# First layer's FFN: up projections of 18 of 22 tiles by a seven-product block scheme, on one NeuronCore

## The chip, the cores and the metric

The kernel runs on one core of one Trainium2 chip. The metric is the device time of one execution in microseconds (us). Before the change it is 2640.16 us, the median of three runs (2639.87 to 2642.24). Five engines work beside each other: TensorE (PE in the profile, its weight loads PEld) multiplies matrices, VectorE (DVE) and ScalarE (ACT) work on elements and can read TensorE's results in PSUM, GpSimd (POOL) works on elements in SBUF and issues some DMAs, and SyncE (SP) issues most DMAs. Each engine runs its own list of instructions in order and waits for others by semaphores.

## The reference

Two layers of a hybrid transformer block, width 1024. Each layer has a token mixer and, after it, the gated feed-forward network (FFN) that the change is about. Layer 1 of the text (index 0 in the code) applies the FFN to 512 latent tokens and 256 context tokens with the same weights, so the kernel handles them as 768 columns; layer 2 applies it to the 512 latent tokens alone.

```python
D_MODEL, SEQ, CTX_LEN, DEPTH = 1024, 512, 256, 2
FFN_HIDDEN = 2816                       # 22 tiles of 128

def swiglu(h, w1, w3, w2):
    return (jax.nn.silu(h @ w1) * (h @ w3)) @ w2

for l in range(DEPTH):
    ...                                 # shift, scale and gate from c @ w_ada[l]; mixer sub-layer
    if not last:
        ctx = ctx + cg_f * swiglu(modulate(rms_norm(ctx, norm_ffn[l]), csh_f, csc_f), w_ffn1[l], w_ffn3[l], w_ffn2[l])
    x = x + g_f * swiglu(modulate(rms_norm(x, norm_ffn[l]), sh_f, sc_f), w_ffn1[l], w_ffn3[l], w_ffn2[l])
return rms_norm(x, final_norm)
```

## The kernel before

**Layout.** Activations stand transposed: 128 channels on the partitions, tokens in the columns. The normalized input h of the FFN is one tile [128, 2, 8, 768]: eight chunks of 128 channels, each twice, as a high part rounded to fp32r and as the remainder, the low part. Weights are split the same way after loading: `wload` (L225) fetches 128x512 pieces (four chunks of one 128-column tile, 256 KB) through SP's queue, and `wsplit` (L218) makes the high part on ScalarE (L220) and the low part on VectorE (L222). There are three buffers for raw pieces and four each for high and low parts. `mm3` (L521 to L527) multiplies by three products per chunk: high by high, high by low, low by high. All accumulate in one PSUM bank.

**The FFN.** `ffn_up` (L1576) makes one of 22 hidden tiles: w1 and w3 columns are loaded and split, then for each of two column halves (0 to 384, 384 to 768) 24 matmuls for the gate, a Silu on ScalarE (L1583), 24 matmuls for the value, the product on VectorE (L1586), and the split of the result into a g tile (L1587, L1588). Five PSUM banks ("f") go round. The hidden tiles form three groups of 8, 7 and 7; after each group a down projection runs over eight column tiles n: it loads w2 for the group's chunks, multiplies them with the g tiles and adds the result, scaled, onto the residual xT (`resid`, L1547). In the first group the first NSF = 3 tiles are done for the latent tokens 0 to 512 first and then for 512 to 768, so that the normalization of the second range hides beside the first. In the last group the down projection runs over all n for columns 0 to 512 and then over all n for 512 to 768; between the two `norm_range` is called on columns 0 to 512 for layer 2's input (a new h tile), so that it runs beside the second range's matmuls. `norm_range` squares and sums on ScalarE and VectorE, sums over partitions on TensorE (L196), takes the power on GpSimd (L169), broadcasts by transposes (L201), and then makes h chunk by chunk (multiply on VectorE, L207; scale and shift, L177, and cast, L180, on ScalarE; low part on VectorE, L181).

**Beside the FFN** runs the modulation of layer 2, `ada_steps` (L111), a generator: each step takes one 128x512 piece of w_ada out of one of two buffers, multiplies it into one or two accumulators on VectorE (L130), and issues the next load on SP's queue (L119). After eight pieces the accumulators are transposed on TensorE (L144) and reduced on VectorE (L145). Three blocks follow each other: the first has two live rows, the others one. `ada_next(n)` takes n steps: NAF = 3 behind each up tile, NAN = 2 inside each down tile n, and what is left before the last down projection.

**Order of work.** Instructions are put into each engine's list by a scheduler that takes, of those that a simulated timeline calls ready, the one that comes first in the program; so work can run ahead of its place where its engine is free and its buffers are. Buffers are given out at the first use and are free after the last. The `ga` tag has six buffers [128, 2, 768] and `gm` eight; they hold the mixer's output for `w_out` and then the g tiles.

```python
groups = [list(range(0, 8)), list(range(8, 15)), list(range(15, 22))]
...
ws = wload(w_ffn2[l], grp_[0] * P, n * P, len(grp_))
ada_next(NAN)
for lo, hi in rngs:
    pu = gbank()[:, :hi - lo]
    mm3(pu, ws, lambda k: gt[k][:, 0, lo:hi], lambda k: gt[k][:, 1, lo:hi])
    resid(pu, n, lo, hi, 40)
```

Of the kernel before, what the change touches and what calls it, by code (L numbers as in the profile page):

```python
# [10 lines left out]
F32 = mybir.dt.float32  # L11
F32R = mybir.dt.float32r
AF = mybir.ActivationFunctionType
# [5 lines left out]
P = 128  # L19
D = 1024  # L20
NC_ = D // P
# [19 lines left out]
NTS = (2, 2)  # L41
AJ = 2
NAF = 3
NAN = 2
NSF = 3
NSL = 4
WB = (0, 3)
PRE = (0.9, 0.9, 0.6, 0.5, 0.5)
# [14 lines left out]
def block_kernel(ctx: ExitStack, tc: tile.TileContext, x, c, ctx_in, c_ctx, w_ada, b_ada, norm_mix, w_in,  # L63
# [12 lines left out]
    def ttile(n=512, name="t"):  # L76
        t = tp.tile([P, 512], F32, tag="t", name=name)
        return t[:, :n]
# [542 lines left out]
    for l in range(DEPTH):  # L621
# [881 lines left out]
        with ExitStack() as st:  # L1503
# [3 lines left out]
            def gbank():  # L1507
                return pf.tile([P, 512], F32, tag="f", name="pf", bufs=5)
# [1 line left out]
            def tbank():  # L1510
                return pf.tile([P, 512], F32, tag="T", name="pT", bufs=2)

            gp.tile([P, 512], F32, tag="tf", name="tf", bufs=2)
            gp.tile([P, 512], F32, tag="wada", name="wada", bufs=4)
            gp.tile([P, 2, NT], F32R, tag="ga", name="g", bufs=6)
            if last:
                deep = {"ws": 8, "wh": 3, "wl": 3}
                for tag, n in deep.items():
# [9 lines left out]
            gcount = [6]  # L1528

            def gtile(name):  # L1530
                i = gcount[0] % 14
# [3 lines left out]
            mg = [gtile("mg") for n in range(NC_)]  # L1535
            xT = []
            for lo, hi in oh:
                for n in range(NC_):
# [29 lines left out]
            def ada_next(n):  # L1568
                for _ in range(n):
                    if ada:  # L1570
                        try:
                            next(ada[0])
                        except StopIteration:
                            ada.pop(0)

            def ffn_up(f, g, rngs):  # L1576
                w1 = wload(w_ffn1[l], 0, f * P, NC_)
                w3 = wload(w_ffn3[l], 0, f * P, NC_)
                for lo, hi in rngs:
                    p1 = gbank()[:, :hi - lo]  # L1580
                    mm3(p1, w1, lambda k: h[:, 0, k, lo:hi], lambda k: h[:, 1, k, lo:hi])
                    t = gp.tile([P, 512], F32, tag="tf", name="tf", bufs=2)[:, :hi - lo]
# [5 lines left out]
                    nc.vector.tensor_sub(g[:, 1, lo:hi], t, g[:, 0, lo:hi])  # L1588

            def finish(lo, hi):  # L1590
                nt = (hi - lo) // P
# [28 lines left out]
                    yield  # L1620

            groups = [list(range(0, 8)), list(range(8, 15)), list(range(15, 22))]
            for gi, grp_ in enumerate(groups):
                gt = []
                for f in grp_:
# [2 lines left out]
                if gi == 0 and last:  # L1628
                    todo = [(grp_[:NSL], [r]) for r in oh] + todo[NSL:]
                elif gi == 0:  # L1630
                    todo = [(grp_[:NSF], [r]) for r in oh] + todo[NSF:]
                for fs, rngs in todo:
                    nr = iter(())
                    if gi == 0 and rngs == [oh[0]]:
                        nr = norm_range(tbank, xT, h, mod, 32, 24, *oh[1])
                        next(nr)
                    for f in fs:
                        ffn_up(f, gt[f - grp_[0]], rngs)
                        next(nr, None)
                    drain(nr)  # L1640
                    if f:
                        ada_next(NAF)
                lastg = gi == len(groups) - 1
                if lastg:
                    for a in ada:
# [80 lines left out]
```

## Time and profile before

| what | value |
|---|---|
| median of three runs | 2640.16 us |
| profiled execution | 2639.56 us |
| its span, first to last instruction | 2637.8 us |
| TensorE busy | 2559.7 us, 14651 matmuls |
| VectorE busy | 1712.7 us |
| ScalarE busy | 1129.8 us |
| GpSimd busy | 114.1 us |
| granted TensorE clock, mean | 0.992 |
| FFN of layer 1, about | 998 to 1553 us of the span |

The profile is of one execution. Busy time is the time in which an engine has an instruction in work; TensorE's matmuls overlap, so their mean durations are longer than the distance of their starts. The span is cut into 40 slices for the digits, 9 is 90% or more busy. The chain that ended last is followed back from the last instruction: at each step to what released it, or to the instruction before it on its engine.

In the FFN of layer 1 the stages are: the first group's tiles for two token ranges until about 1054 us, its other five tiles until 1137, its down projection until 1203, the second group's seven tiles until 1319, its down projection until 1377, the third group's tiles until 1493, the last down projection for columns 0 to 512 until 1533 and for 512 to 768 until 1553.

### The profile page before, as it was taken

The numbers are of one execution on the slowest core, as the hardware profiler recorded it, in microseconds if no ns is written. First come the engines' busy times: TensorE is split into PE (matmuls) and PEld (weight loads), VectorE is DVE, ScalarE is ACT, GpSimd is POOL, SyncE is SP. The second block draws the span as 40 slices with busy tenths as digits, with TensorE's granted clock in tenths as the row PEclk, the third lists the DMA queues.
The fourth block names the chain that finished last, engine by engine and source line by source line (L and its number), as shares of the span: only waits on it lengthen the run. The fifth ranks groups of instructions, "written<-read, shape, count | busy, mean of one in ns | idle before, by whom it ended". The sixth has DMA issues, their size and how long they took to land.

```text
span 2637.8 us, 38763 instructions
## 1 busy us (share of the span) xinstructions
PE 2559.7 (97%) x14651; PEld 2348.8 (89%) x14651; DVE 1712.7 (65%) x3042; ACT 1129.8 (43%) x2262; POOL 114.1 (4%) x179
## 2 busy tenths in 40 slices
PE   7999999999999999999999999999999999999998
PEld 5999889999999988999999988778888888988888
DVE  5967887787778667463453579987766635733335
ACT  5245556556522245212212254566655424722235
POOL 2000000010000000000000000100000000000000
PEclk9999999999999999999999999999999999999999
DMA  8211112222245355343343452111232235633333
GB/s 285 76 41 45 45 33 73 58 62 60 77 150 156 113 164 156 92 128 96 96 152 96 137 148 85 53 41 53 68 80 66 78 96 162 175 96 95 97 92 112
DMA packets 401760, 263.07 MB, mean 100 GB/s; under 512 B 15882, under 2 KB 369492, under 8 KB 401572
## 3 DMA queue, kind: packets, MB, share of 16 engines
q1 hardware_dynamic: 394292, 236.67, 30.3%
q0 software_dynamic: 7280, 23.93, 3.2%
q8 instruction: 115, 1.88, 0.3%
q14 instruction: 73, 0.60, 0.1%
HBM read 243.75 MB, written 8.91 MB: 96 GB/s over the span
## 4 chain that ended last, share of the span: by engine, by line
PE 86%; DVE 5%; ACT 3%; issue 3%; DMA 1%; POOL 0%; DVEq 0%; POOLq 0%; SPq 0%; ACTq 0%
PE pf L527 15%; PE pf L526 14%; PE pf L525 14%; PE pf L609 10%; PE pf L610 10%; PE pf L611 10%; PE pS L906 3%; PE pT L935 2%; PE pv L1345 2%; PE pv L1434 1%; ACT e L925 1%; DVE nm L912 1%; DMA wada<-in_w_ada_dram 1%; ACT rot L798 0%; DVE pt L938 0%
## 5 line engine op out<-in xcount | busy, mean ns | idle before, releaser
L220 ACT CAST wh<-ws 128x512 fp32r<-128x512 f32 (+1 forms) x432 | 260.5, 607 | 564.8 <-PE pf L526 483.3
L526 PE MATMUL pf<-h,wh 128*128 128x384 f32 (+2 forms) x1360 | 468.2, 346 | 0.7 <-DVE h L181 0.6
L525 PE MATMUL pf<-h,wh 128*128 128x384 f32 (+2 forms) x1360 | 466.1, 347 | 2.9 <-ACT tg L730 1.5
L527 PE MATMUL pf<-h,wl 128*128 128x384 f32 (+2 forms) x1360 | 467.0, 346 | 0.0
L609 PE MATMUL pf<-h,wh 128*128 128x384 f32 (+1 forms) x1280 | 459.6, 359 | 1.9 <-ACT tg L781 1.4
L611 PE MATMUL pf<-h,wl 128*128 128x384 f32 (+1 forms) x1280 | 449.1, 351 | 0.0
L610 PE MATMUL pf<-h,wh 128*128 128x384 f32 (+1 forms) x1280 | 448.1, 350 | 0.0
L222 DVE TENSOR_TENSOR wl<-ws,wh 128x512 fp32r<-128x512 f32 (+1 forms) x432 | 288.9, 674 | 243.2 <-ACT wh L220 237.9
L525 PEld LDWEIGHTS pf<-h,wh 128*128 128x128 f32 x1360 | 253.9, 188 | 23.6 <-ACT tg L730 1.7
L526 PEld LDWEIGHTS pf<-h,wh 128*128 128x128 f32 x1360 | 255.8, 188 | 20.7 <-DVE h L181 2.0
L527 PEld LDWEIGHTS pf<-h,wl 128*128 128x128 f32 x1360 | 255.3, 188 | 19.3 <-DVE wl L222 0.2
L565 ACT CAST wh<-ws 128x512 fp32r<-128x512 f32 x264 | 164.1, 623 | 235.1 <-PE pf L610 195.9
L609 PEld LDWEIGHTS pf<-h,wh 128*128 128x128 f32 x1280 | 241.8, 189 | 16.3 <-ACT tg L781 2.0
L610 PEld LDWEIGHTS pf<-h,wh 128*128 128x128 f32 x1280 | 242.0, 189 | 13.4 <-issue 0.7
L611 PEld LDWEIGHTS pf<-h,wl 128*128 128x128 f32 x1280 | 241.2, 188 | 13.4 <-issue 0.2
L572 DVE TENSOR_TENSOR wl<-ws,wh 128x512 fp32r<-128x512 f32 x264 | 181.3, 688 | 97.5 <-ACT wh L565 96.0
L703 DVE SCALAR_TENSOR_TENSOR ca<-ub,cols,ca 128x798 f32<-128x798 f32 (+1 forms) x240 | 215.4, 898 | 3.9
L130 DVE SCALAR_TENSOR_TENSOR wada<-wada,sil 128x512 f32<-128x512 f32 x224 | 162.7, 748 | 56.6 <-DMA wada<-in_w_ada_dram 55.3
L525 PE MATMUL pf<-g,wh 128*128 128x384 f32 (+2 forms) x584 | 198.7, 341 | 0.0
L527 PE MATMUL pf<-g,wl 128*128 128x384 f32 (+2 forms) x584 | 197.5, 339 | 0.7 <-DVE wl L222 0.7
L526 PE MATMUL pf<-g,wh 128*128 128x384 f32 (+2 forms) x584 | 197.3, 338 | 0.0
L937 ACT CAST pt<-pT 128x512 fp32r<-128x512 f32 (+1 forms) x216 | 92.0, 471 | 153.3 <-PE pT L935 152.7
(324 smaller groups left out, 4073.6 us busy)
## 6 DMA issues: line engine op xcount, KB each, us to landing
ws<-in_w_ffn_dram SPq DMA_DIRECT2D x284, 256.0 KB, 3.0
ws<-in_w_in_dram SPq DMA_DIRECT2D x248, 256.0 KB, 2.9
wada<-in_w_ada_dram SPq DMA_DIRECT2D x160, 256.0 KB, 2.9
ws<-in_w_out_dram SPq DMA_DIRECT2D x58, 256.0 KB, 3.5
ws<-in_w_ffn_dram SPq DMA_DIRECT2D x48, 192.0 KB
wada<-in_w_ada_dram SPq DMA_DIRECT2D x16, 512.0 KB, 6.9
khl<-khl POOLq DMA_DIRECT2D x40, 192.0 KB, 3.2
ws<-in_w_four_dram SPq DMA_DIRECT2D x16, 256.0 KB, 2.7
```

The lines of the kernel that those rows point to most:

```text
L130: nc.vector.scalar_tensor_tensor(accs[r], w, s, accs[r], op0=ALU.mult, op1=ALU.add)
L220: nc.scalar.copy(wh[:, :n], st[:, :n])
L222: lastv[0] = nc.vector.tensor_sub(wl[:, :n], st[:, :n], wh[:, :n]).ins
L525: nc.tensor.matmul(o, lhsT=wh, rhs=xh(k), start=(k == 0), stop=False)
L526: nc.tensor.matmul(o, lhsT=wh, rhs=xl(k), start=False, stop=False)
L527: nc.tensor.matmul(o, lhsT=wl, rhs=xh(k), start=False, stop=(k == n - 1))
L565: nc.scalar.copy(wh, u.raw[len(u.wh)])
L572: nc.vector.tensor_sub(wl, u.raw[i], u.wh[i])
L609: nc.tensor.matmul(o, lhsT=wh, rhs=xh(k), start=(k == 0), stop=False)
L610: nc.tensor.matmul(o, lhsT=wh, rhs=xl(k), start=False, stop=False)
L611: nc.tensor.matmul(o, lhsT=wl, rhs=xh(k), start=False, stop=(k == nk - 1))
L703: nc.vector.scalar_tensor_tensor(a, u, w, a, op0=ALU.mult, op1=ALU.add)
```

## The change

In layer 1 (`fast`) hidden tiles 4 to 21 are made in nine pairs by `ffn_pair`, each projection of a pair by `quad`. A quad sees the projection as a 2x2 block product: two output tiles, two halves of the input channels (four chunks each), two halves of 384 columns. Seven products of 4 chunks x 3 matmuls replace eight. On the weight side the sums of blocks (s1, s2, and the later a21 and s2) are made by four GpSimd operations on raw 128x512 pieces; on the activation side `prepare` makes T1 to T4 once from h (T1 in the place of one block of h) with GpSimd, VectorE and ScalarE. The products are put together from PSUM by additions on VectorE and a copy on ScalarE; banks A, B and C take a second or third product by accumulation after they have been read. Raw pieces and sums come from eight buffers (three `ws`, five `sq`). Silu and the product of gate and value work on quarters of 128x384 in a 768-column tile `ts`, and the split into g follows once for the whole tile.

Groups are now 6, 6, 6 and 4 tiles, g tiles have the six `ga` buffers only (the buffers of `gm` go to T2 to T4 and the pieces), and `prepare`'s scratch shares `ga`. The first NCV = 4 tiles are done as before in two token ranges. The modulation takes no step in a pair (NAQ = 0), five in each down tile (NAN = 5), three after each of the two plain passes. Layer 2 runs its FFN as before.

```diff
-NAN = 2
-NSF = 3
+NAN = 5
+NCV = 4
+NAQ = 0
...
+            def prepare():
...
+                def put(dst, v):
+                    nc.scalar.copy(dst[:, 0], v)
+                    nc.vector.tensor_sub(dst[:, 1], v, dst[:, 0])
...
+                t3, t2, t4 = [gp.tile([P, 2, 4, HT], F32R, tag="tb", name="tb", bufs=3) for _ in range(3)]
+                v, u = scratch(), scratch()
+                nc.gpsimd.tensor_sub(u, blk(1, 1, 1), blk(1, 0, 1))
+                nc.vector.tensor_sub(v, blk(0, 1, 1), blk(0, 0, 1))
+                nc.vector.tensor_add(v, v, u)
+                put(t3, v)
+                v2 = scratch()
+                nc.gpsimd.tensor_add(v2, v, blk(1, 0, 0))
+                nc.vector.tensor_add(v2, v2, blk(0, 0, 0))
+                put(t2, v2)
+                u4 = scratch()
+                nc.gpsimd.tensor_sub(u4, blk(1, 1, 0), v2)
+                nc.vector.tensor_add(u4, u4, blk(0, 1, 0))
+                put(t4, u4)
+                nc.gpsimd.tensor_sub(v2, blk(1, 1, 1), v2)
+                nc.vector.tensor_add(v2, v2, blk(0, 1, 1))
+                t1 = h[:, :, 0:4, HT:2 * HT]
+                put(t1, v2)
...
+            def quad(W, f, done):
...
+                a11 = raw(0, f * P)
+                a21 = raw(0, (f + 1) * P)
+                a22 = raw(4 * P, (f + 1) * P)
+                s1 = sqtile("s1")
+                nc.gpsimd.tensor_add(s1, a21, a22)
+                s2 = sqtile("s2")
+                nc.gpsimd.tensor_sub(s2, s1, a11)
+                a12 = raw(4 * P, f * P)
+                w = wsplit(a11, 4)
+                A = gbank()[:, :HT]
+                prod(A, w, tops["B11"], True, True)
+                p1 = ttile(HT, "p1")
+                nc.scalar.copy(p1, A)
+                w = wsplit(s2, 4)
+                nc.gpsimd.tensor_sub(a21, a11, a21)
+                B = gbank()[:, :HT]
+                prod(B, w, tops["T2"], True, True)
+                u2 = ttile(HT, "u2")
+                nc.vector.tensor_add(u2, B, p1)
+                w = wsplit(a12, 4)
+                prod(A, w, tops["B21"], False, True)
+                nc.gpsimd.tensor_sub(s2, a12, s2)
+                done(0, 0, A)
+                w = wsplit(a21, 4)
+                prod(B, w, tops["T3"], False, True)
+                u3 = ttile(HT, "u3")
+                nc.vector.tensor_add(u3, B, p1)
+                w = wsplit(s1, 4)
+                C = gbank()[:, :HT]
+                prod(C, w, tops["T1"], True, True)
+                nc.vector.tensor_add(u3, C, u3)
+                done(1, 1, u3)
+                w = wsplit(a22, 4)
+                prod(B, w, tops["T4"], False, True)
+                nc.vector.tensor_add(p1, B, p1)
+                done(1, 0, p1)
+                w = wsplit(s2, 4)
+                prod(C, w, tops["B22"], False, True)
+                nc.vector.tensor_add(u2, C, u2)
+                done(0, 1, u2)
...
+                quad(w_ffn1, f, gate)
+                ada_next(NAQ)
+                quad(w_ffn3, f, value)
+                ada_next(NAQ)
+                for t, g in zip(ts, (g0, g1)):
+                    nc.scalar.copy(g[:, 0], t)
+                    nc.vector.tensor_sub(g[:, 1], t, g[:, 0])
...
+            if fast:
+                groups = [list(range(0, 6)), list(range(6, 12)), list(range(12, 18)), list(range(18, 22))]
...
-                    todo = [(grp_[:NSF], [r]) for r in oh] + todo[NSF:]
+                    todo = [(grp_[:NCV], [r]) for r in oh]
+                elif fast:
+                    todo = []
...
+                if fast:
+                    if gi == 0:
+                        prepare()
+                    for f in grp_[NCV if gi == 0 else 0::2]:
+                        ffn_pair(f, gt[f - grp_[0]], gt[f + 1 - grp_[0]])
```

## Rows read from the trace of the kernel before

**Rows 1.** The page: TensorE's and others' busy time, TensorE's slices, the chain's shares
```profile
PE 2559.7 (97%) x14651; PEld 2348.8 (89%) x14651; DVE 1712.7 (65%) x3042; ACT 1129.8 (43%) x2262; POOL 114.1 (4%) x179
...
PE   7999999999999999999999999999999999999998
...
PE 86%; DVE 5%; ACT 3%; issue 3%; DMA 1%; POOL 0%; DVEq 0%; POOLq 0%; SPq 0%; ACTq 0%
```
**Rows 2.** Windows by stage: length, busy us (instructions) per engine, clock, DMA, GB/s
```profile
1036.00:1054.00 18.00, 17.74 (x120) 17.42 (x119) 12.05 (x21) 5.93 (x12) 0.00 (x0) 1.00 0.72 215
...
1137.00:1203.00 66.00, 66.00 (x384) 65.85 (x383) 43.39 (x80) 9.49 (x16) 0.00 (x0) 1.00 0.46 140
1203.00:1319.00 116.00, 116.00 (x673) 115.93 (x672) 41.52 (x70) 29.84 (x55) 0.00 (x0) 1.00 0.30 87
1319.00:1377.00 58.00, 58.00 (x336) 57.93 (x335) 35.04 (x65) 9.30 (x16) 0.00 (x0) 1.00 0.52 159
...
1533.00:1553.00 20.00, 19.25 (x157) 18.51 (x156) 13.97 (x27) 11.16 (x20) 2.35 (x3) 1.00 0.55 161
```
**Rows 3.** Timeline of TensorE, up tiles: start us, duration, instruction; 84 starts apart
```profile
1085.17 0.33 PE L525 MATMUL pf<-h,wh 128*128 128x384 f32 x1
...
1099.73 0.33 PE L525 MATMUL pf<-h,wh 128*128 128x384 f32 x1
```
**Rows 4.** Timeline of TensorE, last down projection: three and nine starts apart
```profile
1520.18 0.39 PE L525 MATMUL pf<-g,wh 128*128 128x512 f32 x1
...
1520.88 0.40 PE L525 MATMUL pf<-g,wh 128*128 128x512 f32 x1
...
1539.74 0.28 PE L525 MATMUL pf<-g,wh 128*128 128x256 f32 x1
...
1540.81 0.28 PE L525 MATMUL pf<-g,wh 128*128 128x256 f32 x1
```
**Rows 5.** Groups of VectorE instructions, 1000 to 1640 us: count, busy us, mean ns, idle
```profile
L222 DVE TENSOR_TENSOR wl<-ws,wh 128x512 fp32r<-128x512 f32 x159 | 109.0, 688 | 80.1 <-ACT wh L220 77.1 <-PE pf L527 2.8
L130 DVE SCALAR_TENSOR_TENSOR wada<-wada,sil 128x512 f32<-128x512 f32 x112 | 82.1, 749 | 51.0 <-DMA wada<-in_w_ada_dram 50.5
...
L1588 DVE TENSOR_TENSOR g<-tf,g 128x384 fp32r<-128x384 f32 x38 | 21.1, 556 | 8.7 <-ACT g L1587 8.7
L1586 DVE TENSOR_TENSOR tf<-tf,pf 128x384 f32<-128x384 f32 x38 | 21.0, 554 | 101.2 <-PE pf L527 101.2
...
L1547 DVE SCALAR_TENSOR_TENSOR xT<-pf,mod,xT 128x256 f32<-128x256 f32 x24 | 11.4, 476 | 0.0
L145 DVE TENSOR_REDUCE mod<-pa 128x4 f32<-128x512 f32 x16 | 10.9, 683 | 0.0
L1547 DVE SCALAR_TENSOR_TENSOR xT<-pf,mod,xT 128x384 f32<-128x384 f32 x16 | 9.8, 615 | 10.8 <-PE pf L527 10.8
...
L181 DVE TENSOR_TENSOR h<-hn,h 128x256 fp32r<-128x256 f32 x16 | 6.7, 420 | 0.3 <-ACT h L180 0.2
...
L1547 DVE SCALAR_TENSOR_TENSOR xT<-pf,mod,xT 128x128 f32<-128x128 f32 x16 | 5.6, 347 | 3.6 <-PE pf L527 3.6
```
**Rows 6.** Groups of GpSimd instructions, whole span
```profile
L1290 POOL COPY sb<-ss 128x128 f32<-128x128 f32 x40 | 12.7, 316 | 286.5 <-DVE ss L1288 190.5 <-PE pT L935 63.4 <-PE pS L906 16.4
```
**Rows 7.** Timeline of VectorE: layer 2's modulation in the first down stage
```profile
1132.56 1.42 DVE L130 SCALAR_TENSOR_TENSOR wada<-wada,sil 128x512 f32<-128x512 f32 x2 [1.34 <-DMA wada<-in_w_ada_dram]
...
1136.95 1.41 DVE L130 SCALAR_TENSOR_TENSOR wada<-wada,sil 128x512 f32<-128x512 f32 x2
```
**Rows 8.** Timelines of VectorE and TensorE at the end of the FFN
```profile
1532.23 0.75 DVE L1547 SCALAR_TENSOR_TENSOR xT<-pf,mod,xT 128x512 f32<-128x512 f32 x1 [0.93 <-PE pf L527]
...
1547.71 0.69 DVE L181 TENSOR_TENSOR h<-hn,h 128x512 fp32r<-128x512 f32 x1
...
1556.06 0.47 PE L525 MATMUL pf<-h,wh 128*128 128x512 f32 x1 [0.59 <-ACT hn L177]
```
**Rows 9.** Timeline of VectorE: the last low part of the FFN's h
```profile
1026.42 0.42 DVE L181 TENSOR_TENSOR h<-hn,h 128x256 fp32r<-128x256 f32 x1
```

More of the change, by code (lines that the diff above doesn't have):

```diff
@@ L1511, in tbank @@
                 return pf.tile([P, 512], F32, tag="T", name="pT", bufs=2)
-            gp.tile([P, 512], F32, tag="tf", name="tf", bufs=2)
-            gp.tile([P, 512], F32, tag="wada", name="wada", bufs=4)
-            gp.tile([P, 2, NT], F32R, tag="ga", name="g", bufs=6)
+            fast = not last
+            if fast:
+                for i in range(3):
+                    tbl = gp.tile([P, 2, 4, 384], F32R, tag="tb", name="tb", bufs=3)
+                gp.tile([P, 512], F32, tag="wada", name="wada", bufs=4)
+                gp.tile([P, 4, P], F32, tag="sq", name="sq", bufs=5)
+                gp.tile([P, NTOK], F32, tag="ts", name="ts", bufs=2)
+                gp.tile([P, 2, NT], F32R, tag="ga", name="g", bufs=6)
+            else:
+                gp.tile([P, 512], F32, tag="tf", name="tf", bufs=2)
+                gp.tile([P, 512], F32, tag="wada", name="wada", bufs=4)
+                gp.tile([P, 2, NT], F32R, tag="ga", name="g", bufs=6)
             if last:
@@ L1530, in gtile @@
             def gtile(name):
+                if fast:
+                    return gp.tile([P, 2, NT], F32R, tag="ga", name=name, bufs=6)
                 i = gcount[0] % 14
@@ L1581, in ffn_up @@
                     mm3(p1, w1, lambda k: h[:, 0, k, lo:hi], lambda k: h[:, 1, k, lo:hi])
[L1582 removed]
+                    t = ttile(hi - lo, "tf") if fast else gp.tile([P, 512], F32, tag="tf", name="tf", bufs=2)[:, :hi - lo]
                     nc.scalar.activation(t, p1, AF.Silu)
@@ new lines, in sqtile, with prod @@
+            def sqtile(name):
+                sqn[0] += 1
+                if sqn[0] % 8 < 3:
+                    return wp.tile([P, 4, P], F32, tag="ws", name="ws", bufs=3)
+                return gp.tile([P, 4, P], F32, tag="sq", name=name, bufs=5)
+            sqn = [2]
+            def prod(o, ws, T, start, stop):
+                for k in range(4):
+                    wh, wl = ws[k]
+                    for i, (wt_, x_) in enumerate(((wh, 0), (wh, 1), (wl, 0))):
+                        nc.tensor.matmul(o, lhsT=wt_, rhs=T[:, x_, k], start=(start and k == 0 and i == 0),
+                                         stop=(stop and k == 3 and i == 2), skip_group_check=not start)
@@ new lines, in ffn_pair, with gate, value @@
+            def ffn_pair(f, g0, g1):
+                ts = [gp.tile([P, NTOK], F32, tag="ts", name="ts", bufs=2) for _ in range(2)]
+                def gate(i, j, src):
+                    nc.scalar.activation(ts[i][:, HT * j:HT * (j + 1)], src, AF.Silu)
+                def value(i, j, src):
+                    o = ts[i][:, HT * j:HT * (j + 1)]
+                    nc.vector.tensor_mul(o, o, src)
+                quad(w_ffn1, f, gate)
[5 more added lines that the diff above has]
+                    nc.vector.tensor_sub(g[:, 1], t, g[:, 0])
```

24 lines of the change are left out of this document (23 added, 1 removed).

## The prediction

> **What bounds the kernel now.** I read the page's busy times and slices first, then the chain that ended last. TensorE is busy 97% of the span, 9 tenths in all but two slices, and holds 86% of the chain [rows 1]. So time goes only where matmuls go, or where a new wait opens a hole in TensorE. Then the stages of the changed FFN: TensorE is full in each of them, while VectorE (DVE) fills 36% of the second up stage and 66% of the first down stage [rows 2]. Last the single durations. A matmul's busy time overlaps the next one's, so its price is the distance of starts: 84 starts between 1085.17 and 1099.73 us, 0.1733 us for 384 columns [rows 3]; 0.233 for 512 and 0.119 for 256 [rows 4].
>
> **What is removed.** Two tiles of one projection (I call them a quad) took 2 tiles x 8 chunks x 3 products x 2 halves = 96 matmuls of 384 columns, 16.64 us. Now they take 7 x 4 x 3 = 84, 14.56 us. There are 9 pairs, so 18 quads and 216 matmuls less: **37.4 us**. The down projections keep their number of matmuls. One more tile goes by 512 and 256 columns instead of twice 384 (48 x 0.005 = 0.3 us more), and three chunks of eight column tiles leave that split in the last group (72 x 0.005 less): nothing together.
>
> **What is added inside a quad.** ScalarE is 26% busy in the second up stage [rows 2]; three more casts and a copy fit. DVE has seven weight subtractions at 0.688 and five additions out of PSUM, priced as the 384-column product of gate and value, 0.554: 7.6 us for the gate. The value quad adds four products at 0.554 and two g subtractions of 768 columns (0.556 plus 384 more at 1.0 ns, the step from 420 ns at 256 to 688 at 512, so 0.94): 11.7 us [rows 5]. Mean 9.6 of 14.56 us, where the same work had 5.0 of 16.64. DVE is two thirds full, so not the bound by its sum, but each quad hands PSUM banks back and forth: before products 3, 4, 6 and 7 a copy or addition must have read the bank, and only one product, 12 x 0.1733 = 2.08 us, lies between. Behind one weight subtraction the addition needs 0.69 + 0.55 = 1.24 us, which is in time.
>
> GpSimd gets four 128x512 additions a quad. The trace has no such instruction. Nearest below is DVE's of the same shape, 0.69 us. Above is GpSimd's 128x128 copy, 316 ns [rows 6], times four for the elements and two for the second input, 2.53. I take 1.26, four copies, since that row is GpSimd's own. At four a quad, 5.0 of 14.56 us, it hides; its results are wanted some products later. A subtraction that such an addition holds up makes the hand-over 1.26 + 1.24 = 2.50, late by 0.42. Of the 72 hand-overs (four in each quad) I take one in eight as late: **4 us** (0 to 30, all late).
>
> **What is added once: prepare.** Four GpSimd and five DVE operations and four splits over 1536 columns. Per DVE operation 0.556 + 1152 x 1.0 ns = 1.71 us; GpSimd 12 x 0.316 = 3.8 (1.71 to 7.6). T2, needed by the second product, hangs on two GpSimd operations, three on DVE and a cast of about 1.7: 14.4 us in a row (10 to 22). h is complete at 1026.8 us [rows 9]; the four plain tiles end near 1066 (their 4 x 48 x 0.352 = 67.6 us begin about 998.5). The chain fits in these 39 us, but DVE is 67% busy in their second half, from 1036 to 1054 [rows 2], which leaves 13 us for 15.4 us of it. The rest runs beside the first quad, where T1 and T4 are due some 8 to 11 us later: **3 us** (0 to 14, the T2 chain uncovered).
>
> **What is moved: the modulation of layer 2.** Its 106 steps stood three behind each up tile and two in each down tile. Now six stand beside the plain tiles, none in quads, five in each down tile: 40 in a down stage of 8 x 36 x 0.1733 = 49.9 us. In the first one DVE has 27 chunks x 2 x 0.749 = 40.4, eight reductions 5.5, six chunks of the next block 4.5, weight splits 8 x (0.69 + 0.42) = 8.9, residuals 8 x (0.615 + 0.476 + 0.347) = 11.5 [rows 5]: 70.8 us. A chunk also waits for its own 256 KB load: two chunks in 4.4 us where they run without a break [rows 7], and 27 at that pace take 59. SP carries them ahead of the first quads' weight loads. So some 21 us of DVE work spill over into the next quads, which have 4.9 us to spare each. There two of these multiplies in front of an addition make 1.50 + 1.24 = 2.74, late by 0.66; over the ten or so products in the overflow **6 us** (0 to 21, the whole spill on the path). The second down stage has 51 us of DVE work by the same count (single multiplies now), the third 14 less: nothing. The 24 more residuals (11.5 us of DVE) lie within these sums.
>
> **What loses its cover: the end of this FFN.** In the last group the second token range, 256 columns, hides the first range's normalization. It had 8 x 7 x 3 = 168 matmuls, 19.9 us; with four tiles it has 96, 11.4 us. The first h chunk was complete at 1548.4, 16 us after the last residual began at 1532.2, and TensorE already waits for ScalarE's h at 1556.06, 0.59 us [rows 8]; its busy share in that stretch is 19.25 of 20 us [rows 2]. 8.5 us of cover are gone. Half the weight splits between are gone too, which lets the normalization run faster: **5 us** (0 to 8.5). At the other group ends the last gated tile passes through one 768-column cast and subtraction; four earlier chunks hide that.
>
> **Sum.** Made against the profiled execution, 2639.56 us (span 2637.8, 1.8 around it): 2639.6 - 37.4 + 4 + 3 + 6 + 5 = 2620.2. The median of the runs is 0.6 higher, so I forecast 2621.
>
> **A rule weighed.** Rows show DVE additions with nothing large on GpSimd, so no contention can be read in them. The Trainium skill, SBUF — State Buffer, section "SBUF: two separate sides", says that a GpSimd operation and a DVE one with two SBUF inputs exclude each other for the whole instruction. No run here shows it yet; it would be the last rival below. For the GpSimd addition itself the Trainium skill, GPSIMD Engine Reference, section "3.1 Elementwise — side-by-side cycle accounting", gives 4497 ns at 2048 columns, an estimate of 1.1 us at 512; by it the sum stays as it is.
>
> **Rivals.**
> *Everything is covered.* For it: TensorE idles under 0.3 us in each stage but the last though DVE reaches 67% [rows 2], weights are split up to four products ahead, and all added work fits by its sums. Against it: the lost cover at the end of the FFN, which no buffer replaces. Then 2640.2 - 37.4 + 0 to 5 = 2603 to 2608.
> *The spill is on the path.* The modulation comes first in program order, its transposes sit in TensorE's own queue, and quads wait behind it. For it: 70.8 against 49.9 us. Against it: the same chain ran at the same pace in the stage from 1137 with TensorE full [rows 2]. 21 us instead of 6: 2636, no measurable change or barely faster.
> *DVE and GpSimd take turns, and DVE becomes the bound of the quads.* If each GpSimd addition holds DVE for its length P, a quad takes 9.6 + 4P: over 14.56 from P = 1.23 us. For it: P may be up to 2.53, and well over half of DVE's quad time is subtractions of two SBUF tiles. Against it: the additions out of PSUM and DVE's gaps can lie beside GpSimd. At P = 1.9, midway between 1.26 and 2.53, it is 17.2, 2.7 us more in each of 18: 2640.2 - 37.4 + 14 + 48 = 2665, slower. It decides from P = 1.55, where the 23 us that are left are used up.
> That the change doesn't do what it says I exclude: the product count stands in the loops.
>
> **Chances.** Forecast (2608 to 2633) 0.50; everything covered 0.24; spill on the path (2633 to 2646) 0.14; turns (over 2646) 0.12. A difference under 0.2%, 5.3 us, can't be told from none here. Of the spill's 0.14, 0.02 is faster, 0.10 the same, 0.02 slower. Faster 0.76, same 0.10, slower 0.14. The range 2602 to 2646 leaves out the last rival and a little at the low end.
>
> **What would show it.** In the profile after: 84 matmuls a quad and 216 matmuls fewer; starts in a quad 0.173 apart with short waits on DVE's or ScalarE's reading of PSUM at the third, fourth, sixth or seventh product; a hole of some us before layer 2's first matmuls that wait for h; TensorE's waits in the first quads after the first down stage; GpSimd's 128x512 additions near 1.3 us. The forecast is wrong if TensorE is full through the quads and the hole at the end of the FFN is missing (then faster), or if DVE's weight subtractions are much longer than 0.69 us while GpSimd runs (then slower).

## The result, and the profile after

The changed kernel takes 2664.69 us, the median of four runs (2659.73 to 2665.27), against 2640.56 for the kernel before beside it: a ratio of 1.0086 (95% interval 1.0069 to 1.0104). It is slower; forecast were 2621 us and a range of 2602 to 2646. The profiled execution took 2665.27 us, its span 2663.3.

The page after, whose lines answer to [rows 1]: span, busy time of each engine, TensorE's busy tenths in 40 slices, the chain by engine.

```profile
span 2663.3 us, 38749 instructions
PE 2548.0 (96%) x14435; PEld 2328.1 (87%) x14435; DVE 1852.1 (70%) x3205; ACT 1171.7 (44%) x2324; POOL 237.2 (9%) x255
PE   7999999999999998898999999999999999999998
PE 80%; DVE 8%; issue 4%; DMA 4%; ACT 3%; SPq 0%; POOL 0%; DVEq 0%; POOLq 0%; ACTq 0%
```

The matmuls are 14435, 216 fewer, as counted. The price stands in the three slices with an 8 ahead of the last, from 999 to 1132 and from 1198 to 1265 us, and in VectorE's share of the chain. To place it I took from both timelines the start of each stage (its first matmul behind the last one of the stage ahead) and set each stage's length against its matmuls times the distances of [rows 3, 4]. What is left I call "over": TensorE waits, runs at its lower clock, or transposes for the modulation. The last two columns are from windows of these stages: the time in which TensorE is idle, and its granted clock.

| stage of this FFN, after | from, to (us) | length | its matmuls | over | idle | clock |
|---|---|---|---|---|---|---|
| 4 plain tiles, first pair, first down | 990.8, 1170.3 | 179.5 | 146.6 | 32.9 | 17.2 | 0.94 |
| 3 pairs, second down | 1170.3, 1331.8 | 161.5 | 137.3 | 24.2 | 12.6 | 0.97 |
| 3 pairs, third down | 1331.8, 1478.8 | 147.0 | 137.3 | 9.7 | 3.7 | 0.99 |
| 2 pairs, last down, to layer 2's first matmul | 1478.8, 1578.5 | 99.7 | 92.0 | 7.7 | 5.4 | 0.99 |

Before, its three groups were over by 4.8, 2.7 and 5.7, idle for 1.7 in all, at a clock of 1.00. So 74.5 - 13.2 = 61.3 us of new loss stand against 550.8 - 513.2 = 37.6 us of matmuls removed. With a start 1.3 earlier and a layer 2 that is 3.1 longer (1084.8 against 1081.7 us to the end) the span grows by 25.5 us, as measured. Of the 61.3 us, 37 are TensorE's new idle time; a good part of the rest is a slower clock (last section).

Windows of the kernel after (length, then PE, PEld, DVE, ACT and POOL busy with their instructions, granted clock, DMA share, GB/s): the prepare with the first pair, the first down projection, the second group's quads, then on into the third's. The last two lines are 10 us each inside quads of the third and fourth groups.

```profile
1026.00:1100.00 74.00, 56.84 (x305) 50.95 (x305) 71.61 (x79) 25.01 (x41) 24.20 (x8) 0.86 0.43 127
1100.00:1180.00 80.00, 78.25 (x454) 77.75 (x453) 63.18 (x107) 19.44 (x36) 9.85 (x7) 1.00 0.39 117
1180.00:1290.00 110.00, 99.12 (x538) 95.64 (x537) 90.93 (x139) 36.68 (x65) 32.45 (x22) 0.95 0.50 151
1290.00:1400.00 110.00, 106.29 (x595) 104.16 (x595) 76.96 (x127) 31.98 (x57) 24.36 (x17) 0.98 0.41 121
1400.00:1410.00 10.00, 10.00 (x59) 10.00 (x59) 8.55 (x13) 4.95 (x8) 4.38 (x3) 1.00 0.17 49
1510.00:1520.00 10.00, 10.00 (x59) 10.00 (x58) 8.55 (x13) 4.96 (x8) 4.38 (x3) 1.00 0.12 35
```

From 1026 to 1100 VectorE is busy 71.6 of 74 us and TensorE is idle for 17. In the last two lines a quad runs with GpSimd busy 44% and TensorE has not one gap: a quad by itself costs what its 84 matmuls do. No multiply of the modulation lies in these two windows. What the first windows have beside a quad is the modulation and the prepare.

What TensorE waits for from 1026 to 1170 and, below, from 1170 to 1332 (its line, whose result on which engine and line, us in total, times, longest). L528 and L1658 are matmuls of the plain tiles and of the quads, L223 is the weight split's subtraction, L1692 an addition out of PSUM in a quad:

```profile
PE pf L528 <- DVE wl L223: 8.2, 7, 2.7
PE pf L1658 <- DVE wl L223: 4.5, 3, 2.9
...
PE pf L1658 <- DVE wl L223: 5.0, 4, 2.2
PE pf L1658 <- DVE u L1692: 3.3, 1, 3.3
```

Groups of VectorE's and GpSimd's instructions, 1000 to 1640 us (count, busy us, mean ns, idle time before them). L131 is the modulation's multiply, L1672 a sum of weight blocks. The first two answer to [rows 5], 749 and 688 ns there.

```profile
L131 DVE SCALAR_TENSOR_TENSOR wada<-wada,sil 128x512 f32<-128x512 f32 x112 | 103.1, 935 | 25.0 <-DMA wada<-in_w_ada_dram 24.6
L223 DVE TENSOR_TENSOR wl<-ws,wh 128x512 fp32r<-128x512 f32 x133 | 99.8, 753 | 30.1 <-ACT wh L221 29.1 <-PE pf L528 1.1
L1704 DVE TENSOR_TENSOR u<-pf,u 128x384 f32<-128x384 f32 x18 | 10.0, 555 | 15.6 <-PE pf L1658 15.6
L1672 POOL TENSOR_TENSOR s<-s,sq 128x512 f32<-128x512 f32 x4 | 5.2, 1295 | 7.7 <-DVE wl L223 7.7
```

VectorE's instructions that read two SBUF tiles got longer, those that read PSUM did not. Here is why, in one quad: VectorE's and then GpSimd's timeline (start, duration, instruction, idle before it), first at 1245 us, last in the prepare at 1060.

```profile
1245.84 1.52 DVE L131 SCALAR_TENSOR_TENSOR wada<-wada,sil 128x512 f32<-128x512 f32 x1
1060.27 3.93 DVE L223 TENSOR_TENSOR wl<-ws,wh 128x512 fp32r<-128x512 f32 x1
```

```profile
1245.54 1.28 POOL L1687 TENSOR_TENSOR s<-sq,s 128x512 f32<-128x512 f32 x1 [9.75 <-DVE wl L223]
1060.19 3.46 POOL L1636 TENSOR_TENSOR sc<-h,sc 128x1536 f32<-128x1536 f32 x1 [7.86 <-DVE sc L1633]
```

The multiply began 0.30 us into a GpSimd addition that ended at 1246.82 and itself ended 0.54 after that, at 1247.36; the weight subtraction began 0.08 after a GpSimd subtraction that ended at 1063.65 and ended at 1064.20. I call that holding. From 1020 to 1560 us, 49 instructions of VectorE are over 0.1 us longer than the median of their form, 47.4 us together, and each lies beside a GpSimd operation of the change.

### The profile page after: what moved, and what is told of

It reads as the page before. It is cut to its first block, busy times and chain, and to the rows that moved or that the text cites. A ratio compares the mean times of both kernels' runs of the same rounds, so it can differ in the third digit from the quotient of the medians.

```text
span 2663.3 us, 38749 instructions
## 1 busy us (share of the span) xinstructions
PE 2548.0 (96%) x14435; PEld 2328.1 (87%) x14435; DVE 1852.1 (70%) x3205; ACT 1171.7 (44%) x2324; POOL 237.2 (9%) x255
## 4 chain that ended last, share of the span: by engine, by line
PE 80%; DVE 8%; issue 4%; DMA 4%; ACT 3%; SPq 0%; POOL 0%; DVEq 0%; POOLq 0%; ACTq 0%
PE pf L610 10%; PE pf L611 10%; PE pf L612 10%; PE pf L528 10%; PE pf L527 10%; PE pf L526 10%; PE pf L1658 8%; PE pS L907 3%; PE pT L936 2%; DMA wada<-in_w_ada_dram 2%; PE pv L1346 2%; PE pv L1435 1%; DVE wl L223 1%; DVE wada L131 1%; DMA ws<-in_w_in_dram 1%
## 5 line engine op out<-in xcount | busy, mean ns | idle before, releaser
L221 ACT CAST wh<-ws 128x512 fp32r<-128x512 f32 (+2 forms) x407 | 242.2, 600 | 531.1 <-PE pf L527 370.4
L223 DVE TENSOR_TENSOR wl<-ws,wh 128x512 fp32r<-128x512 f32 (+2 forms) x407 | 277.1, 686 | 186.9 <-ACT wh L221 183.0
L528 PE MATMUL pf<-h,wl 128*128 128x512 f32 (+2 forms) x784 | 279.1, 359 | 8.2 <-DVE wl L223 8.2
L526 PE MATMUL pf<-h,wh 128*128 128x512 f32 (+2 forms) x784 | 277.1, 360 | 8.8 <-ACT h L181 5.3
L527 PE MATMUL pf<-h,wh 128*128 128x512 f32 (+2 forms) x784 | 279.3, 359 | 1.0 <-DVE h L182 0.9
L610 PEld LDWEIGHTS pf<-h,wh 128*128 128x128 f32 x1280 | 241.6, 189 | 16.3 <-ACT tg L782 2.0
L611 PEld LDWEIGHTS pf<-h,wh 128*128 128x128 f32 x1280 | 241.8, 189 | 13.4 <-issue 0.6
L612 PEld LDWEIGHTS pf<-h,wl 128*128 128x128 f32 x1280 | 241.0, 188 | 13.3 <-issue 0.2
L131 DVE SCALAR_TENSOR_TENSOR wada<-wada,sil 128x512 f32<-128x512 f32 x224 | 183.6, 840 | 30.5 <-DMA wada<-in_w_ada_dram 28.9
L528 PE MATMUL pf<-g,wl 128*128 128x384 f32 (+2 forms) x584 | 196.1, 339 | 0.0
L526 PEld LDWEIGHTS pf<-h,wh 128*128 128x128 f32 x784 | 148.3, 192 | 31.5 <-ACT h L181 7.9
L528 PEld LDWEIGHTS pf<-h,wl 128*128 128x128 f32 x784 | 150.2, 192 | 29.4 <-DVE wl L223 10.0
L527 PEld LDWEIGHTS pf<-h,wh 128*128 128x128 f32 x784 | 150.1, 192 | 23.5 <-DVE h L182 4.2
```

What stands on the lines that cost most here:

```text
L131: nc.vector.scalar_tensor_tensor(accs[r], w, s, accs[r], op0=ALU.mult, op1=ALU.add)
L221: nc.scalar.copy(wh[:, :n], st[:, :n])
L223: lastv[0] = nc.vector.tensor_sub(wl[:, :n], st[:, :n], wh[:, :n]).ins
L526: nc.tensor.matmul(o, lhsT=wh, rhs=xh(k), start=(k == 0), stop=False)
L527: nc.tensor.matmul(o, lhsT=wh, rhs=xl(k), start=False, stop=False)
L528: nc.tensor.matmul(o, lhsT=wl, rhs=xh(k), start=False, stop=(k == n - 1))
```

## The experiments

Four theories. **L** (lock): GpSimd's additions hold VectorE, and that is the loss. **M** (modulation): packing its steps into the down tiles is the loss. **S** (sum): from 1026 to about 1290 us VectorE has prepare, modulation, weight splits and holding to fit in, each fits alone, together they don't; taking any of them away gives much back. **E** (end): the lost cover in the last group matters. Later came **P** (place): the prepare stands beside the plain tiles' second token range, where a 128x512 weight piece feeds only 12 matmuls of 256 columns (12 x 0.119 = 1.43 us) and its split takes 0.69 of VectorE. All ratios are to the kernel before.

### e1_sums_on_vector: all 76 GpSimd operations of the change on VectorE

```diff
-                nc.gpsimd.tensor_add(s1, a21, a22)
+                nc.vector.tensor_add(s1, a21, a22)
```
(and so for the other seven lines in `prepare` and `quad`)

> All 76 GpSimd additions and subtractions of the change (72 weight sums, 4 in the preparation of T1 to T4) are done by VectorE instead; nothing else differs. Theory L (lock: a GpSimd addition holds VectorE's instructions with two SBUF inputs for its length, 49 of them stretched by 47 us in all): no weight subtraction or modulation multiply is stretched any more, means back at 0.69 and 0.75 us from 0.75 and 0.94; VectorE gets 72 x 0.69 + 4 x 1.75 = 57 us of work and loses 47, so its busy time is about 1862 us. If only the sum of its work counts, the time is 2655 to 2670; if it is the holding at moments that the order of the lists did not foresee, 2635 to 2650. Theory M (the modulation that runs in and ahead of the down stages fills VectorE, GpSimd is a side matter): 2660 to 2675, VectorE full from 1040 to 1095 us as before.

Ratio 0.9995 (0.9986 to 1.0005): 24 us of the loss are gone, with no modulation moved. M by itself is out (2660 to 2675); 2637 us lies in the range for holding at moments that the lists did not foresee. The same groups in this kernel:

```profile
L131 DVE SCALAR_TENSOR_TENSOR wada<-wada,sil 128x512 f32<-128x512 f32 x112 | 81.9, 745 | 18.6 <-DMA wada<-in_w_ada_dram 18.1
L223 DVE TENSOR_TENSOR wl<-ws,wh 128x512 fp32r<-128x512 f32 x133 | 90.8, 685 | 30.8 <-ACT wh L221 29.6 <-PE pf L528 1.1
```

The durations are those of [rows 5] again. VectorE's busy time stays what it was, 1853.4 us against 1852.1: 76 more instructions cost it what the holding had cost. So the sum of its busy time isn't what differs; a held instruction falls where it falls, with the rest of the list behind it, and the GpSimd result is late too (additions that wait for VectorE took up to 3.73 us instead of 1.28).

### e2_no_weight_sums: the 72 sums of the quads left out

```diff
-                nc.gpsimd.tensor_add(s1, a21, a22)
-                nc.gpsimd.tensor_sub(s2, s1, a11)
+                s1 = a22
+                s2 = a11
...
-                nc.gpsimd.tensor_sub(a21, a11, a21)
...
-                nc.gpsimd.tensor_sub(s2, a12, s2)
+                s2 = a12
```

> Leaves out the 72 weight sums of the quads: the products use raw weight pieces in their place; the 4 GpSimd operations of the preparation stay, matmuls, splits and loads are the same in number. Theory L: of VectorE's 47 us of stretching some 34 go; TensorE's lost time in the second and third pair groups (21 and 4 us) mostly goes, the loss of 25 us beside the preparation stays for the most part: 2636 to 2648. Theory M: both losses stay, 2655 to 2665.

1.0009 (0.9999 to 1.0019), as theory L had it. Without the sums, the prepare's four GpSimd operations and the modulation still take the whole gain of 37 us. The second and third groups, 33.9 us over in the change (table above), are 15.0 over here and 15.2 in e1: the same 72 sums in VectorE's own list cost those groups no more than leaving them out.

### e3_mod_behind_prepare: the modulation waits for the prepare

```diff
-                    nc.vector.tensor_sub(dst[:, 1], v, dst[:, 0])
+                    lastn[0] = nc.vector.tensor_sub(dst[:, 1], v, dst[:, 0]).ins
...
-                    if f:
+                    if f and not fast:
                         ada_next(NAF)
```

> The modulation of layer 2 takes no step beside the four plain tiles, and its VectorE multiplies are ordered behind the last instruction of the preparation; down stages keep five steps a tile. Theory M: VectorE is relieved of some 26 us between 1026 and 1095 us, so of the 25 us that TensorE loses there at most 8 stay; the second pair group loses a few us more than its 21, as nine steps more stand in the down stages: 2642 to 2652. Theory L: GpSimd's four long operations hold VectorE there whatever it has to do, so the loss falls by less than 10: 2655 to 2662.

1.0041 (1.0026 to 1.0056): 12 us back, with all GpSimd operations in place, in the range that M gave.

### e4_mod_spread: two steps a down tile, three behind each quad

```diff
-NAN = 5
-NAQ = 0
+NAN = 2
+NAQ = 3
```

> Undoes the move of the modulation: two steps in each down tile instead of five, three behind each quad instead of none (six behind each pair, as six stood behind two tiles before). Theory M: the second and third pair groups' loss (25 us) falls by at least 15, the loss beside the preparation stays: 2640 to 2650. Theory L: the quads now have modulation and GpSimd sums side by side in all groups, so the held time grows to 55 us or more and each group loses: 2664 to 2680.

1.0088 (1.0073 to 1.0103), no change; 2661 us lies in neither range. Whether the steps stand in the down tiles or behind the quads isn't the cause.

### e5_mod_one_piece: one of eight pieces of the modulation

```diff
-        chunks = [(q, k) for q in range(4) for k in range(NC_)]
+        chunks = [(q, k) for q in range(4) for k in range(1 if l else NC_)]
```

> Leaves out seven of every eight pieces of layer 2's modulation (their loads and all 112 multiply-adds, 103 us of VectorE's busy time in the changed kernel); GpSimd's sums and the rest stay. Theory S (sum: VectorE has more to do between 1026 and 1290 us than the time there, and preparation, modulation and holding by GpSimd are three loads that add up): with the largest load gone TensorE loses under 8 us up to 1290 instead of 46, the hole at the end of the FFN stays: 2608 to 2622. Theory L (the holding by itself stalls TensorE): 2640 to 2655, as 76 GpSimd instructions still hold VectorE.

0.9944 (0.9929 to 0.9959): 37 us back, and every GpSimd operation still there. Its second and third groups take 139.1 us each for 137.3 of matmuls, while its weight subtractions are held (790 ns in the group's row). So holding alone costs the quads next to nothing: L alone falls, as M alone does by e1. S said 2608 to 2622; it became 2623.9. One thing is not parted here: with the multiplies the loads of w_ada are gone too. SP issues these in its own list, among the weight loads, and in the change it stood 82.2 us between 1020 and 1290 us with such a load until a multiply had freed its buffer, 37.3 in the kernel before. What is left, about 16 us, lies from 1040 to 1100. The wait with its cause there, on TensorE, VectorE and GpSimd:

```profile
1057.22 0.58 PE L528 MATMUL pf<-h,wl 128*128 128x256 f32 x1 [4.35 <-DVE wl L223]
```

```profile
1053.28 4.49 DVE L223 TENSOR_TENSOR wl<-ws,wh 128x512 fp32r<-128x512 f32 x2
```

```profile
1053.19 3.43 POOL L1636 TENSOR_TENSOR sc<-h,sc 128x1536 f32<-128x1536 f32 x1 [6.59 <-DVE sc L1633]
```

A GpSimd subtraction of the prepare holds the weight split that TensorE's second token range needs next.

### e6_prepare_on_vector: the prepare's four GpSimd operations alone

```diff
-                nc.gpsimd.tensor_sub(u, blk(1, 1, 1), blk(1, 0, 1))
+                nc.vector.tensor_sub(u, blk(1, 1, 1), blk(1, 0, 1))
```
(and the other three of `prepare`)

> The four 1536-column GpSimd operations of the preparation go to VectorE (4 x 1.75 = 7 us more work, the 12.7 us for which they held other instructions gone); the 72 weight sums stay on GpSimd. Theory S: VectorE gets 6 us in the stretch to 1100 us, so the time falls by 3 to 8: 2655 to 2661. Theory L: the long holds of 3 us each are what TensorE's 25 us there come from: 2640 to 2650.

1.0063 (1.0045 to 1.0082). The interval overlaps that of the change, so by itself this shows nothing sure; 2656.5 us lies in the range of S.

### e7_groups_4666: the small group first

```diff
-                groups = [list(range(0, 6)), list(range(6, 12)), list(range(12, 18)), list(range(18, 22))]
+                groups = [list(range(0, 4)), list(range(4, 10)), list(range(10, 16)), list(range(16, 22))]
```

> The groups are 4, 6, 6 and 6 tiles instead of 6, 6, 6 and 4, all else as in the changed kernel. The last group's second token range gets 144 matmuls of 256 columns instead of 96, 5.7 us more cover for the normalization, and the preparation stands beside the first down projection (192 matmuls) rather than ahead of the first pair. Theory E (the end of the FFN lost its cover): the hole of 5.5 us before layer 2's first matmuls falls under 1.5 and the slow ramp behind it by half. Theory S: the loss up to 1290 us changes by less than 10 either way, as VectorE's work in sum is the same: together 2645 to 2660. If the loss beside the preparation hangs on its place, below 2640.

1.0073 (1.0058 to 1.0088), by its time not to be told from the change; the wait itself is plain. Layer 2's first matmul, after:

```profile
1578.46 0.80 PE L526 MATMUL pf<-h,wh 128*128 128x512 f32 x1 [5.30 <-ACT h L181]
```

and with six tiles in the last group, with the one new wait ahead of it:

```profile
1566.48 0.58 PE L526 MATMUL pf<-g,wh 128*128 128x256 f32 x1 [1.60 <-ACT wh L221]
1575.15 0.47 PE L526 MATMUL pf<-h,wh 128*128 128x512 f32 x1 [1.09 <-DVE ub L721]
```

5.30 us of waiting for h become 1.09, put down to another VectorE instruction, and 2.1 come back in the second range as waits for weight splits (this one and one of 0.49). The last group as a whole is 9.5 us over its matmuls, 7.7 in the change: E shows in this wait and not in the group's time.

### e8_vector_behind_4666: e1, e3 and e7 together

> Three changes at once: all sums on VectorE (first experiment), modulation behind the preparation and out of the plain tiles (third), groups 4, 6, 6, 6 (as above). Theory S: the gains partly add up, 28 + up to 16 + 6 or more off 2664: 2612 to 2626, faster than the kernel before. If they are the same microseconds taken away twice: 2630 to 2637.

0.9961 (0.9947 to 0.9975), 2630.2 us: the range for the same microseconds taken away twice. Singly the three gave 24, 12 and 3 us, together 33. TensorE is still not full in the prepare, where nothing of GpSimd is left:

```profile
1050.00:1060.00 10.00, 6.63 (x52) 6.02 (x50) 10.00 (x12) 5.54 (x10) 0.00 (x0) 1.00 0.44 129
1060.00:1070.00 10.00, 7.91 (x55) 7.19 (x56) 10.00 (x12) 4.44 (x7) 0.00 (x0) 1.00 0.35 100
```

VectorE is full on the prepare's 1536-column operations, and plain tiles' weight splits wait in its list. This is where P comes from.

### e10_vector_early and e11_prepvec_early: modulation ahead of the FFN; sums on VectorE or on GpSimd

Both are e8 with the modulation begun before `w_out`; e11 has the 72 sums of the quads on GpSimd, and the prepare alone on VectorE.

```diff
-NAN = 5
+NAN = 4
...
                         resid(pu, n, lo, hi, 16)
+                    ada_next(2)
```

> The three changes of the eighth experiment, and the modulation of layer 2 begins in the output projection ahead of the FFN, where VectorE has time: two steps behind each of its 13 passes (26 of 109 steps), four instead of five in each down tile. Theory S (VectorE's sum of work in the FFN): some 35 us of multiplies leave the FFN, TensorE's loss in the pair groups (about 15 us) falls under 5: 2614 to 2622. If the order of the lists, not the load, makes what is left: no change, 2628 to 2634.

> As the run before, but the 72 weight sums are on GpSimd again (the preparation stays on VectorE). Theory S: VectorE has 50 us of sums less and some 30 us of holding more, so about the same or a little faster: 2610 to 2624. Theory L (holding costs more than the same work in VectorE's own list, since the order of the lists can't allow for it): 5 to 15 us slower than the run before.

e10: 0.998 (0.997 to 0.999); the FFN begins 7 us later, VectorE being busy 65 of 80 us beside `w_out` from 920 to 1000. e11: 1.0047 (1.0029 to 1.0064). S missed both: 2632.6 us is the time given for the order of the lists, and e11 is slower where S said as fast or faster. They differ in 72 instructions' engine alone, by 17.5 us. TensorE's waits from 1000 to 1400 us, e10 then e11:

```profile
PE pf L1659 <- DVE u L1693: 0.6, 1, 0.6
```

```profile
PE pf L1659 <- DVE u L1693: 7.0, 5, 2.3
```

That is the reading of a PSUM bank between two products (L1692 after), an instruction that is never held (558 ns at most). In each of the five waits it stands right behind a multiply of the modulation, itself not lengthened; in four of them that multiply first waited 1.3 to 2.1 us for its piece of w_ada. The first, on e11's VectorE:

```profile
1132.99 0.75 DVE L131 SCALAR_TENSOR_TENSOR wada<-wada,sil 128x512 f32<-128x512 f32 x1 [2.01 <-DMA wada<-in_w_ada_dram]
1133.66 0.55 DVE L1693 TENSOR_TENSOR u<-pf,p 128x384 f32<-128x384 f32 x1
```

TensorE loses only under load, as e11's windows show: quads of the second group and the start of its down projection, with modulation, and a stretch of the third group, with next to none.

```profile
1180.00:1240.00 60.00, 55.57 (x315) 53.55 (x314) 51.30 (x82) 19.33 (x34) 11.93 (x8) 1.00 0.52 158
...
1300.00:1360.00 60.00, 59.62 (x340) 58.47 (x339) 45.52 (x66) 24.90 (x44) 24.96 (x18) 1.00 0.25 72
```

Twice as much GpSimd work in the second costs TensorE 0.4 us; in the first it loses 4.4 (2.9 in waits for weight splits, 0.9 for this addition), where e10's TensorE is busy 59.8. From 1060 to 1180 us e11's granted clock falls to 0.91 to 0.97, and e10's is 1.00, so a part of the 17.5 us is the clock.

### e12_vector_early_after_plain and e13_vector_after_plain: the prepare behind the plain tiles

The prepare's work is ordered behind the last g subtraction of the plain tiles; e12 is e10 with that, e13 is e8 with that (no early modulation). In e13 the modulation, ordered behind the prepare as in e8, moves along: its first multiply stands at 1102.6 us instead of 1074.6.

```diff
-                    nc.vector.tensor_sub(g[:, 1, lo:hi], t, g[:, 0, lo:hi])
+                    plain[0] = nc.vector.tensor_sub(g[:, 1, lo:hi], t, g[:, 0, lo:hi]).ins
...
-                        prepare()
+                        with tc.issue_after(plain[0]):
+                            prepare()
```

> As the tenth, and VectorE's part of the preparation is ordered behind the last g subtraction of the four plain tiles, so that it stands beside the first down projection alone. Theory P (the second token range of the plain tiles, 256 columns a weight piece, already takes half of VectorE's time for the weight subtractions, so the preparation must not stand there): the loss up to 1080 us, about 6 in the eighth experiment, falls under 2, at most 3 appear before the first pair: 3 to 5 us faster than the tenth. Otherwise the T2 chain of some 15 us comes too late for the first pair: 3 to 8 slower.

> The eighth experiment with VectorE's part of the preparation ordered behind the four plain tiles, and without the early start of the modulation, which in the tenth run made layer 1's FFN begin 7 us later (1000.8 instead of 993.6 us) and so gave back what the pair groups won. If place of the preparation and place of the modulation act by themselves: the eighth run less the 8 us that the twelfth gained on the tenth: 2618 to 2625, clearly faster than the kernel before. If the preparation's gain needs a VectorE relieved of the modulation: 2626 to 2632.

0.9942 (0.9923 to 0.9962) and 0.992 (0.9906 to 0.9933), each 0.4% below the kernel without it, as P said (e12 by more than it said). e13, 2617.76 us in the median, beats the kernel before by 0.8% and the change by 1.7%. Its page and the plain tiles' window in which TensorE was busy 6.63 us in e8:

```profile
PE 2531.0 (97%) x14435; PEld 2313.7 (88%) x14435; DVE 1857.8 (71%) x3289; ACT 1174.8 (45%) x2332; POOL 114.5 (4%) x179
```

```profile
1050.00:1060.00 10.00, 10.00 (x86) 10.00 (x85) 5.91 (x11) 5.20 (x10) 0.00 (x0) 1.00 0.61 174
```

## Why the prediction was wrong

**Right:** the 216 matmuls and their 37.4 us; GpSimd's price, 1.28 to 1.30 us unheld at 512 columns for 1.26 forecast, and 3.46 to 4.12 at 1536 for 3.8; the end of the FFN, forecast 5: the wait for h is 5.30 us against the 0.59 of [rows 8], and the last stage and layer 2 together are 2.0 + 3.1 longer; and the hand-overs of a quad left to itself, which cost not 4 us but nothing.

**The first step that failed** is "The chain fits in these 39 us" with its 3 us (0 to 14). That stage went from 4.8 to 32.9 us over: 28. The room was misread. The plain tiles began at 992 us in the kernel before, not 998.5, so four of them end near 1060 and leave 33 us, not 39. Their second token range, matmuls of 256 columns, ran there from 1025 to 1043 us and not until about 1054, as the section on the time before has it. So the window of [rows 2], 1036 to 1054, shows 7 us of that range and 11 of the full tiles behind it. TensorE's timeline and the range's own window, before:

```profile
1025.02 0.28 PE L525 MATMUL pf<-h,wh 128*128 128x256 f32 x1
...
1043.15 0.34 PE L525 MATMUL pf<-h,wh 128*128 128x384 f32 x1
```

```profile
1026.00:1043.00 17.00, 16.93 (x141) 16.73 (x140) 16.68 (x30) 7.80 (x16) 0.00 (x0) 1.00 0.74 219
```

VectorE was busy 16.68 of 17 us there, not 67%, with 8.15 us of it in multiplies of the modulation. The 13 us that I found for 15.4 us of prepare were not there, and I left six modulation steps in the stage besides. Above all I asked when T2 is due, not whose work the prepare stands in front of: the plain tiles' own weight splits, due every 1.43 us. e13 against e8 prices that place at 0.4%, 11 us, the modulation's later start included: the stage (there four plain tiles and their down projection) is 7.5 us over in e8 and not over at all in e13. In the changed kernel's order e1, e3 and e5 take 9, 14 and 11 us off the 32.9, together more than the 28 that were lost.

**The second** is the modulation's "6 us" with the "4 us" for hand-overs. The second and third groups came out 24.2 and 9.7 us over, where the second before was 2.7. The spill I had reckoned, some 21 us, was right in kind, but I set it against the quads' spare time of 4.9 us each as if nothing else used that. Holding used it, and the multiplies also wait in the list for their own loads (24.6 us in the group's row; 50.5 in [rows 5], with TensorE full), now with additions behind them: the 3.3 us wait for `u` above ends so. TensorE's and VectorE's timelines:

```profile
1187.69 1.01 PE L1658 MATMUL pf<-tb,wh 128*128 128x384 f32 x2 [3.25 <-DVE u L1692]
```

```profile
1184.02 0.74 DVE L131 SCALAR_TENSOR_TENSOR wada<-wada,sil 128x512 f32<-128x512 f32 x1
1184.68 0.68 DVE L146 TENSOR_REDUCE mod<-pa 128x4 f32<-128x512 f32 x1
1186.33 0.75 DVE L131 SCALAR_TENSOR_TENSOR wada<-wada,sil 128x512 f32<-128x512 f32 x1 [0.97 <-DMA wada<-in_w_ada_dram]
...
1187.09 0.55 DVE L1692 TENSOR_TENSOR u<-pf,p 128x384 f32<-128x384 f32 x1
```

The addition that frees the PSUM bank stands behind two multiplies, a reduction and the wait for a piece of w_ada.

**The third** is how holding was placed: in a rival, as a price for each quad, and not in the sum. "Turns" gave the right time, 2665, by luck, for a mechanism that is only half right. With the measured P of 1.29 it makes 9.6 + 5.2 = 14.8 us a quad, 0.2 over the matmuls, near nothing, and quads alone confirm that. VectorE is held and loses 47 us, but TensorE loses only where the list has no slack. The Trainium skill, SBUF — State Buffer, section "SBUF: two separate sides", states the exclusion, and the trace agrees: all 49 lengthened instructions lie beside a GpSimd one, and none of the additions out of PSUM is among them though 30 lay beside one. TensorE's clock had no term either; the last section puts it at some 14 us, an estimate.

So prepare, modulation and holding were each priced against the same free time of VectorE, which was there once at most. That they act together shows in the second and third groups: 33.9 us over in the change, 15.2 with the sums on VectorE (e1), 3.6 with most of the modulation gone and all sums on GpSimd (e5). The sums on GpSimd cost 19 us beside the modulation and under 4 without it. But S fails as a plain sum of VectorE's busy time, by e10, by e11 and by the groups of e1 and e2. What counts is which late instruction stands in the list ahead of one that TensorE waits for.

What stays open: how much of the 17.5 us between e10 and e11 is VectorE's held instructions, how much the GpSimd sums' own lateness, how much the loads of w_ada and the clock; no run parts them. Nor was it tried to win the rest: e13 gains 20 of the 37 us (2638.15 to 2617.76), and its second to fourth groups are still 12.1, 9.8 and 6.6 us over.

## What to carry to other kernels

When several edits each lean on an engine's free time, make one account of that time by stage and take every edit out of it in turn; what fits alone says nothing of the sum. Take the stage's borders from the instructions themselves: here a window 10 us late made 98% look like 67%. Work on GpSimd beside VectorE isn't free work: before moving sums there, see whether VectorE's own instructions in that stage read SBUF alone, and how late its list may run. A one-off preparation belongs where the instructions behind it in its engine's list are due late, not where the engine looks least busy.

## What the runs showed of the hardware

A VectorE instruction that reads one SBUF tile, and a factor for each partition, was held as well. On VectorE's timeline, two multiplies that start a modulation block, beside GpSimd's first operation of the prepare; two of them took 4.13 us (the first 0.48, the second 3.74).

```profile
1025.59 4.13 DVE L133 TENSOR_SCALAR wada<-wada,sil 128x512 f32<-128x512 f32 x2
```

```profile
1025.80 3.63 POOL L1627 TENSOR_TENSOR sc<-h 128x1536 f32<-128x1536 f32 x1 [18.02 <-issue]
```

And TensorE's clock suffered too. From 1020 to 1030 us TensorE was busy without a gap; then (windows as above):

```profile
1030.00:1040.00 10.00, 9.60 (x62) 8.58 (x60) 8.39 (x14) 2.17 (x4) 0.00 (x0) 1.00 0.65 193
1040.00:1050.00 10.00, 7.41 (x37) 7.12 (x38) 10.00 (x14) 2.90 (x6) 1.54 (x1) 0.66 0.53 149
1050.00:1060.00 10.00, 5.32 (x39) 4.50 (x38) 10.00 (x11) 3.47 (x6) 2.33 (x1) 1.00 0.40 114
```

With the first waits the granted clock falls to a mean of 0.66, so for part of the window to the lower of its levels, 1.2 of 2.4 GHz; the next, with longer waits, has 1.00 again and more matmuls in less busy time. So a part of the loss in the prepare is a slower clock, which the prediction had no term for.

It isn't the prepare alone. From 990.8 to 1578.5 us the granted clock was at the lower level for some 37 us in all, and TensorE was busy in 31 of them; in the kernel before it was not there at all in this FFN. It fell eight times, each time during a wait of TensorE of 1.8 to 5.3 us or within 1.4 us behind it. After the wait of 3.25 us shown above six starts of 384 columns lie 1.92 us apart, so 0.32 us each instead of 0.1733:

```profile
1188.49 0.52 PE L1658 MATMUL pf<-tb,wl 128*128 128x384 f32 x1
...
1190.41 0.52 PE L1658 MATMUL pf<-tb,wl 128*128 128x384 f32 x1
```

At that rate the 31 us cost some 14, an estimate, of the 61.3. So some waits cost time twice, as idle time and as slow matmuls behind them.
